# The low-rank projections of the attention at the head of a two-block kernel, on the raw input

## The chip, the cores and the metric

The kernel runs on one core of a Trainium2 chip. The metric is the time of one execution on the device in microseconds; the number to compare is the median of several executions.

## The reference, cut to what matters

The input `x` has 512 tokens of 1024 features in fp32. A first block holds a gated delta rule, latent attention and a feed-forward part; a second block holds a state space layer and a short convolution. Only the head of the first block bears on the change:

```
h = rmsnorm(x, norm_mix_g)                 # x * rsqrt(mean(x*x) + 1e-6) * g
z = h @ w_in
qkv_a, gate_a, a_a, b_a, c_q, c_kv, k_pe, gate_br_a, gate_br_b = split_in(z)
qkv_a = silu(causal_dwconv(qkv_a))         # delta rule: q, k, v of 8 heads
...                                        # chunked, with a triangular solve
cq  = rmsnorm(c_q,  mla_q_norm_g)          # 384 wide
q_b = cq @ w_uq
ckv = rmsnorm(c_kv, mla_kv_norm_g)         # 256 wide
kv  = ckv @ w_ukv
```

`rmsnorm` multiplies each token (row) by one factor. `c_q` and `c_kv` go through a second `rmsnorm` of their own, and a factor that is common to a row cancels there but for the `1e-6` under the root.

## The kernel before, in words

Activations are kept transposed, features on the partitions and the 512 tokens on the free axis, as tiles of 128x512. A product of 1024 input features to 128 output features is eight blocks of weights; since fp32 is split into a high and a low part (`hi`, `lo`), each block costs three matmuls `hi,hi`, `lo,hi`, `hi,lo`, 24 for a product, which add up in one PSUM bank. TensorE has four such banks for products (tiles `mm`) and four for everything else (`pt`). Weights come as chunks of eight blocks in exactly the order of the products (`order`, `pack_weights`): a chunk is loaded into `raw`, ScalarE writes its `hi`, VectorE or GpSimd its `lo`.

Each engine works off its own queue in order. The order is fixed when the program is built: tasks written as generators are advanced by `drive`, and `idle` hands some operations to VectorE or to GpSimd by an estimated clock. The product order is a hand-written table: `START`, then a few fixed products, then `GDN_ORDER`. In it `kq` is the k and q product of a delta-rule head, `vg` its v and gate, `bra` and `brb` two gates of the merge, `low` the three `cq` and two `ckv` products, `att` a head of the attention, `wv` its values, `ya` the first product behind the delta rule.

At the start the row factor `rs` of the first norm isn't known until all eight tiles of `x` have come. So the first products work on `x * gain` ("folded", `self.fold`), and what leaves PSUM is multiplied by `rs`: one VectorE operation `z<-mm,rs` for each product, behind which the convolution of a k or q product follows (one ScalarE and three VectorE operations), and then silu. `t_rs` computes `rs` (`meanrs`, `bcast`) and normalises the eight tiles (`x<-x,rs`), which are split again (`hi<-x,gmix` on ScalarE, `lo<-x,gmix,hi` on VectorE). From `unfold` on the products use these. The four products of `START` go block by block side by side, so they finish together. `ab` holds the decay and beta of the delta rule and the rotary key; `t_gates` runs a softplus on it (`sp_*`, `gg`), whose result TensorE sums (`pt<-gg,sqc`).

In a head of the delta rule `t_gdn_a` prepares k and q; for four heads together `t_solve` inverts triangular 32x32 blocks in 31 steps of two operations (`st<-sl,sx`, `sx<-sx,st`), in groups of four steps of which each goes to VectorE or to GpSimd; `t_gdn_b` carries the state through the four chunks of 128 tokens, from the tile `X` on, and ends in the tile `ga`. `ya` needs all eight `ga`.

`low` makes the five products from normalised tiles and copies each out of PSUM (`lr<-mm`, ScalarE); `t_rank_norm` then squares, adds and normalises them.

## Time and profile before

| | us |
|---|---|
| median of 3 runs | 1483.94 (1483.07 to 1485.86) |
| the profiled execution | 1485.18 |
| its span, first to last instruction | 1483.2 |
| TensorE busy | 1449.1 (98%) |
| VectorE busy | 864.5 (58%) |
| ScalarE busy | 655.1 (44%) |
| GpSimd busy | 503.9 (34%) |

The page's chain of what ended last is TensorE for 85% and VectorE for 10% of the span. A matmul's busy time in the trace is longer than its share of the engine, since matmuls overlap; the distance between the starts of two says more.

### The profile page before, as it was taken

What the parts mean: (1) busy time and instruction counts of PE and PEld (TensorE: products, weight loads), DVE (VectorE), ACT (ScalarE), POOL (GpSimd) and SP (SyncE); (2) the same over time, 40 slices, a digit from 0 to 9 for tenths busy, and PEclk for the clock granted to TensorE, in tenths of its full rate; (3) what the DMA queues carried; (4) which work ended last, traced back from release to release, by engine and by line L of the source; (5) the groups of instructions that cost most, each with busy time, mean ns of one, the idle gap of its engine ahead of it and who ended that gap; (6) DMA issues with size and microseconds to landing.
All of it is one profiled execution on the core that took longest, in us unless ns stands there. A gap on an engine that the chain in (4) does not pass through costs nothing.

```text
span 1483.2 us, 18958 instructions
## 1 busy us (share of the span) xinstructions
PE 1449.1 (98%) x7084; PEld 1191.0 (80%) x7084; DVE 864.5 (58%) x1755; ACT 655.1 (44%) x1118; POOL 503.9 (34%) x284
## 2 busy tenths in 40 slices
PE   8699999999999999999999999999999999999998
PEld 6588788878888888888888888888787778878877
DVE  7978988798665454358441144346975564360073
ACT  4565345234566664345442244444544544442342
POOL 0213010201333424442654455544024435534421
PEclk9799999999999999999999999999999999999999
DMA  5144323331222224423333333333233433422322
GB/s 192 50 147 127 117 82 96 87 86 58 80 79 78 79 72 128 147 94 100 99 99 99 90 96 99 94 96 94 71 104 114 118 115 98 137 86 85 105 85 94
DMA packets 56890, 147.61 MB, mean 100 GB/s; under 512 B 15008, under 2 KB 15584, under 8 KB 56800
## 3 DMA queue, kind: packets, MB, share of 16 engines
q1 hardware_dynamic: 56800, 146.42, 32.6%
q8 instruction: 55, 0.90, 0.2%
q14 instruction: 35, 0.29, 0.1%
HBM read 139.48 MB, written 5.34 MB: 98 GB/s over the span
## 4 chain that ended last, share of the span: by engine, by line
PE 85%; DVE 10%; DMA 2%; issue 1%; POOL 1%; ACT 1%; SPq 0%; DVEq 0%; POOLq 0%; ACTq 0%
PE mm L243 76%; PE pt L243 9%; DVE lo L243 3%; DVE st L243 1%; DVE sx L243 1%; DVE k L243 0%; DVE q L243 0%; SPq L243 0%; DVE rq_u L243 0%; DVE mix L243 0%; DMA raw<-wstream 0%; DVE v L243 0%; DVE xr L243 0%; DVE x L243 0%; ACT hi L243 0%
## 5 line engine op out<-in xcount | busy, mean ns | idle before, releaser
L243 PE MATMUL mm<-hi,hi 128*128 128x512 f32 (+2 forms) x1872 | 744.9, 398 | 5.6 <-ACT hi L243 3.5
L243 PE MATMUL mm<-lo,hi 128*128 128x512 f32 (+2 forms) x1872 | 729.1, 390 | 8.6 <-DVE lo L243 8.6
L243 PE MATMUL mm<-hi,lo 128*128 128x512 f32 (+2 forms) x1872 | 728.8, 390 | 3.9 <-DVE lo L243 3.9
L243 POOL TENSOR_TENSOR lo<-raw,hi 128x1024 fp32r<-128x1024 f32 x149 | 358.8, 2408 | 580.4 <-ACT hi L243 559.7
L243 PEld LDWEIGHTS mm<-hi,lo 128*128 128x128 f32 x1872 | 353.7, 189 | 78.9 <-DVE lo L243 5.1
L243 PEld LDWEIGHTS mm<-hi,hi 128*128 128x128 f32 x1872 | 354.3, 189 | 76.6 <-ACT hi L243 6.7
L243 PEld LDWEIGHTS mm<-lo,hi 128*128 128x128 f32 x1872 | 354.6, 189 | 76.1 <-DVE lo L243 10.3
L243 ACT ACTIVATE hi<-raw 128x1024 fp32r<-128x1024 f32 (+1 forms) x230 | 242.2, 1053 | 225.3 <-PE mm L243 172.1
L243 DVE TENSOR_TENSOR lo<-raw,hi 128x1024 fp32r<-128x1024 f32 (+1 forms) x81 | 102.6, 1267 | 2.6 <-ACT hi L243 2.5
L243 DVE TENSOR_TENSOR sq<-sq,sq 128x512 f32<-128x512 f32 x43 | 32.6, 770 | 93.0 <-ACT sq L243 93.0
L243 DVE TENSOR_TENSOR xr<-xr,mm 128x512 f32<-128x512 f32 x24 | 16.5, 688 | 97.5 <-PE mm L243 97.5
L243 DVE TENSOR_TENSOR lo<-fu,hi 128x512 fp32r<-128x512 f32 x22 | 43.0, 1956 | 41.5 <-ACT hi L243 41.5
L243 DVE SCALAR_TENSOR_TENSOR fu<-mm,params,fu 128x510 f32<-128x510 f32 (+1 forms) x38 | 28.5, 749 | 62.6 <-ACT fu L243 61.9
L243 POOL TENSOR_TENSOR q<-q,row 128x512 f32<-128x512 f32 x8 | 10.4, 1294 | 157.9 <-PE pt L243 92.5
L243 ACT ACT_TABLE_LOAD x37 | 47.5, 1283 | 8.3 <-DVE xbc L243 2.6
L243 POOL TENSOR_TENSOR fu<-fg,fu 128x512 f32<-128x512 f32 x22 | 30.0, 1365 | 44.9 <-DVE fu L243 41.3
L243 DVE TENSOR_TENSOR lo<-scz,hi 128x512 fp32r<-128x512 f32 x8 | 15.8, 1969 | 32.7 <-ACT hi L243 32.7
L243 DVE TENSOR_TENSOR lo<-pt,hi 128x512 fp32r<-128x512 f32 (+3 forms) x32 | 15.6, 489 | 28.9 <-ACT hi L243 28.8
L243 DVE SCALAR_TENSOR_TENSOR fg<-mm,params,fg 128x510 f32<-128x510 f32 (+1 forms) x38 | 28.3, 744 | 6.2 <-ACT fg L243 5.5
L243 ACT ACTIVATE fg<-fg 128x512 f32<-128x512 f32 x22 | 13.9, 631 | 39.4 <-DVE fg L243 39.4
L243 POOL TENSOR_TENSOR xdd<-xd,dd 128x512 f32<-128x512 f32 x8 | 9.4, 1176 | 58.7 <-DVE xd L243 58.6
L243 DVE TENSOR_SCALAR row<-row,cmp 128x128 f32<-128x128 f32 x64 | 26.9, 487 | 0.0
(314 smaller groups left out, 1513.9 us busy)
## 6 DMA issues: line engine op xcount, KB each, us to landing
raw<-wstream SPq DMA_DIRECT2D x228, 512.0 KB, 3.6
row<-grow_d SPq DMA_DIRECT2D x16, 256.0 KB, 4.2
row<-crow_d SPq DMA_DIRECT2D x16, 256.0 KB, 4.8
x<-xT SPq DMA_DIRECT2D x8, 256.0 KB, 5.4
sbd<-gate SPq DMA_DIRECT2D x8, 256.0 KB, 2.1
sb<-sbd SPq DMA_DIRECT2D x8, 256.0 KB, 3.9
xr<-xT SPq DMA_DIRECT2D x8, 256.0 KB, 3.8
Ce<-crow_d SPq DMA_DIRECT2D x16, 128.0 KB, 4.8
```

The lines of the kernel that those rows point to most:

```text
L243: return f(*args, **kw)
```

## The change

The five products `cq` and `ckv` move to the very start and work on `x * gain`; they are copied out of PSUM without `rs`. Their norm gets `epsx`, the mean square of the input (with its epsilon) times `1e-6`, in place of `1e-6`, so that the missing factor cancels exactly. `ab` still gets `rs`. The k and q products of heads 0 to 2 come behind `unfold`, from normalised tiles, the first three side by side. `low` now only starts the two norms. `GDN_ORDER` is another one; the last products ahead of `ya` are the same set.

```
-START = ["ab", ("k", 0), ("q", 0), ("k", 1)]
-GDN_ORDER = [("brb", 0), ("vg", 0), ("kq", 3), ("brb", 1), ("brb", 2), ("kq", 4), ...
+START = ["ab", ("cq", 0), ("cq", 1), ("cq", 2)]
+FIRST = [("k", 0), ("q", 0), ("k", 1)]
+GDN_ORDER = [("brb", 0), ("kq", 3), ("brb", 1), ("brb", 2), ("kq", 4), ("brb", 3), ("vg", 0), ...
...
-    o = [START] + one([("q", 1), ("k", 2), ("q", 2)])
+    o = [START] + one([("ckv", 0), ("ckv", 1)]) + [FIRST] + one([("q", 1), ("k", 2), ("q", 2)])
...
-                    nc.vector.tensor_scalar(a, cs, 1.0 / n, eps, ALU.mult, ALU.add)
+                    if isinstance(eps, float):
+                        nc.vector.tensor_scalar(a, cs, 1.0 / n, eps, ALU.mult, ALU.add)
+                    else:
+                        nc.vector.scalar_tensor_tensor(a, cs, 1.0 / n, eps, ALU.mult, ALU.add)
...
     def t_rs(self, x, n, gain, keep, eng=None):
-        r = yield from self.meanrs(x, n, eng=eng)
+        nc = self.nc
+        a = yield from self.meansq(x, n, eng=eng)
+        r = yield from self.rsqrt(a, NC)
         self.rs = yield from self.bcast(r, "rs")
+        if not keep:
+            self.epsx = self.const.tile([128, NC], F32, name="epsx")
+            nc.vector.tensor_scalar(self.epsx, a, EPS, None, ALU.mult)
...
-        r = yield from self.meanrs(raw, 128 * n)
+        a = yield from self.meansq(raw, 128 * n, eps=self.epsx)
+        r = yield from self.rsqrt(a, NC)
...
+        raws = {"cq": [None] * 3, "ckv": [None] * 2}
+
         def low():
-            for key, n, gname in (("cq", 3, "mla_q_norm_g"), ("ckv", 2, "mla_kv_norm_g")):
-                raw = [None] * n
-                for m in range(n):
-                    ps = yield from self.linear((key, m), self.xh)
-                    self.spawn(self.t_rows(raw, m, ps, None, "lr"))
-                self.spawn(self.t_rank_norm(key, raw, gname))
+            for key, gname in (("cq", "mla_q_norm_g"), ("ckv", "mla_kv_norm_g")):
+                self.spawn(self.t_rank_norm(key, raws.pop(key), gname))
...
         ps = yield from self.linears(START, self.xh)
         self.spawn(t_ab(ps[0]))
-        yield from kq(0, ps[1], ps[2])
+        for m in range(3):
+            self.spawn(self.t_rows(raws["cq"], m, ps[1 + m], None, "lr"))
+        for m in range(2):
+            ps = yield from self.linear(("ckv", m), self.xh)
+            self.spawn(self.t_rows(raws["ckv"], m, ps, None, "lr"))
+        yield from self.unfold()
+        ps = yield from self.linears(FIRST, self.xh)
+        yield from kq(0, ps[0], ps[1])
...
         yield from kq(2)
-        yield from self.unfold()
```

Three places show how the queues move. First, TensorE and ScalarE at the end of `START`, which is `mm17` here; TensorE before (`mm59` is q of head 1, `mm14` is `ab`):

```order
L243 MATMUL mm17_137<-lo42_223,hi3_221 128x512
L243 MATMUL mm17_137<-hi39_209,lo3_231 128x512
L243 MATMUL pt53_346<-sqc_75,rs50_322 128x128 [waits DVE_49]
L243 MATMUL pt53_346<-sqc_75,rs50_322 128x128 x3
L243 MATMUL mm59_361<-hi18_138,hi4_262 128x512 [waits DVE_49,Activation_49]
L243 MATMUL mm59_361<-lo20_142,hi4_262 128x512
```

TensorE now (`mm56` is the first `ckv` product):

```order
L244 MATMUL mm17_137<-lo42_223,hi3_221 128x512
L244 MATMUL mm17_137<-hi39_209,lo3_231 128x512
L244 MATMUL mm56_348<-hi18_138,hi4_262 128x512 [waits Activation_49]
L244 MATMUL mm56_348<-lo20_142,hi4_262 128x512
L244 MATMUL mm56_348<-hi18_138,lo4_273 128x512
L244 MATMUL mm56_348<-hi22_146,hi4_262 128x512
L244 MATMUL mm56_348<-lo28_159,hi4_262 128x512
L244 MATMUL mm56_348<-hi22_146,lo4_273 128x512
L244 MATMUL pt57_363<-sqc_75,rs50_322 128x128 [waits DVE_49]
L244 MATMUL pt57_363<-sqc_75,rs50_322 128x128 x3
L244 MATMUL mm56_348<-hi26_154,hi4_262 128x512
```

ScalarE before, and now:

```order
L243 ACTIVATE hi5_295<-raw5_290 128x1024 [waits DMAHW1_49,DVE_49,PE_49]
L243 COPY rs54_351<-pt53_346 128x512 [waits PE_49]
L243 ACTIVATE hi6_364<-raw6_362 128x1024 [waits DMAHW4_49,DVE_49]
L243 ACTIVATE hi63_378<-x4_103,gmix_112 128x512 [waits DVE_49]
L243 ACTIVATE cmp_393<-gyb67_390 128x4x8 [waits DVE_49]
```

```order
L244 ACTIVATE hi5_295<-raw5_290 128x1024 [waits DMAHW1_49,DVE_49,PE_49]
L244 COPY lr53_343<-mm15_135 128x512 [waits PE_49]
L244 COPY lr54_345<-mm16_136 128x512 [waits PE_49]
L244 COPY lr55_347<-mm17_137 128x512 [waits PE_49]
L244 ACTIVATE hi6_358<-raw6_349 128x1024 [waits DMAHW2_49,DVE_49]
L244 COPY rs58_368<-pt57_363 128x512 [waits PE_49]
L244 ACTIVATE hi63_395<-x4_103,gmix_112 128x512 [waits DVE_49]
```

The transposes that spread `rs` (`pt<-sqc,rs`) stood directly behind `START` and stand six matmuls later now; the next product waited for VectorE to empty the bank of `ab`, and now for ScalarE's copy of `mm15`, a `cq` product. On ScalarE three copies and the `hi` of a chunk stand ahead of the copy of `rs`.

Second, the softplus of the gates. VectorE ahead of it before (`k74`, `q75`, `k78` are convolutions, `x4` to `x11` the tiles of the input, `lo86` belongs to the rotary key):

```order
L243 SCALAR_TENSOR_TENSOR k74_409<-z60_372,params_74,k74_409 128x509 [waits Activation_49]
L243 SCALAR_TENSOR_TENSOR k74_409<-z60_372,params_74,k74_409 128x510 [waits DVE_49]
L243 SCALAR_TENSOR_TENSOR k74_409<-z60_372,params_74,k74_409 128x511 [waits DVE_49]
L243 TENSOR_TENSOR x8_107<-x8_107,rs54_351 128x512
L243 SCALAR_TENSOR_TENSOR q75_414<-z61_374,params_74,q75_414 128x509 [waits Activation_49]
L243 SCALAR_TENSOR_TENSOR q75_414<-z61_374,params_74,q75_414 128x510 [waits DVE_49]
L243 SCALAR_TENSOR_TENSOR q75_414<-z61_374,params_74,q75_414 128x511 [waits DVE_49]
L243 SCALAR_TENSOR_TENSOR k78_426<-z62_376,params_74,k78_426 128x509 [waits Activation_49]
L243 SCALAR_TENSOR_TENSOR k78_426<-z62_376,params_74,k78_426 128x510 [waits DVE_49]
L243 SCALAR_TENSOR_TENSOR k78_426<-z62_376,params_74,k78_426 128x511 [waits DVE_49]
L243 TENSOR_TENSOR lo86_489<-rot77_424,hi80_448 64x512 [waits Activation_49]
L243 TENSOR_TENSOR lo87_492<-rot77_424,hi80_448 64x512
L243 TENSOR_SCALAR sp_s70_399<-sp_e69_398 128x32 [waits Activation_49]
```

VectorE now:

```order
L244 TENSOR_TENSOR x7_106<-x7_106,rs58_368 128x512
L244 SCALAR_TENSOR_TENSOR lo74_430<-x5_104,gmix_112,hi65_405 128x512
L244 TENSOR_TENSOR x8_107<-x8_107,rs58_368 128x512
L244 SCALAR_TENSOR_TENSOR lo81_462<-x6_105,gmix_112,hi75_432 128x512 [waits Activation_49]
L244 TENSOR_TENSOR x9_108<-x9_108,rs58_368 128x512
L244 TENSOR_SCALAR sp_s71_422<-sp_e70_421 128x32 [waits Activation_49]
```

TensorE at the sum of the gates, before (`mm95` is the first product from normalised tiles) and now (`mm88` to `mm90` are k and q of head 0 and k of head 1):

```order
L243 MATMUL mm90_523<-hi39_209,lo6_382 128x512
L243 MATMUL pt97_573<-gg88_513,sqc_75 128x32 [waits DVE_49,PE_49]
L243 MATMUL pt97_573<-gg88_513,sqc_75 128x32
L243 MATMUL mm95_567<-hi63_378,hi7_476 128x512 [waits Activation_49]
L243 MATMUL mm95_567<-lo64_380,hi7_476 128x512
L243 MATMUL mm95_567<-hi63_378,lo7_538 128x512 [waits DVE_49]
```

```order
L244 MATMUL mm89_511<-hi75_432,lo6_373 128x512
L244 MATMUL pt95_556<-gg82_483,sqc_75 128x32 [waits DVE_49,PE_49]
L244 MATMUL pt95_556<-gg82_483,sqc_75 128x32
L244 MATMUL mm90_512<-hi75_432,hi7_485 128x512 [waits Activation_49]
L244 MATMUL mm90_512<-lo81_462,hi7_485 128x512
L244 MATMUL mm90_512<-hi75_432,lo7_507 128x512 [waits DVE_49]
L244 MATMUL mm88_510<-hi80_457,hi7_485 128x512
```

Nine convolution operations stood directly ahead of the softplus (`sp_s`), and none does now; all convolutions of heads 0 to 2 stand behind the split of the last input tile. On TensorE the sum stood ahead of the first product from normalised tiles and now stands behind 24 matmuls of it.

Third, GpSimd at the first solve, before and now (`q194` is a q tile, `X218` and `X228` are tiles `X`, `lo17` and `lo24` chunks of weights):

```order
L243 TENSOR_TENSOR st192_1250<-sl188_1202,sx189_1203 64x112 [waits Pool_49]
L243 TENSOR_TENSOR sx189_1203<-sx189_1203,st192_1250 64x28x4 [waits Pool_49]
L243 TENSOR_TENSOR lo17_1268<-raw17_1224,hi17_1259 128x1024 [waits DVE_49,DMAHW3_49,PE_49,Activation_49]
L243 MEMSET X218_1612 128x512
L243 MEMSET X228_1647 128x512
L243 TENSOR_TENSOR q194_1276<-q194_1276,row224_1637 128x512 [waits DMAHW3_49,PE_49,Activation_49]
```

```order
L244 TENSOR_TENSOR st194_1360<-sl190_1316,sx191_1317 64x112 [waits Pool_49]
L244 TENSOR_TENSOR sx191_1317<-sx191_1317,st194_1360 64x28x4 [waits Pool_49]
L244 TENSOR_TENSOR st194_1360<-sl190_1316,sx191_1317 64x247 [waits DVE_49,Pool_49]
L244 TENSOR_TENSOR sx191_1317<-sx191_1317,st194_1360 64x19x13 [waits Pool_49]
L244 TENSOR_TENSOR st194_1360<-sl190_1316,sx191_1317 64x252 [waits Pool_49]
L244 TENSOR_TENSOR sx191_1317<-sx191_1317,st194_1360 64x18x14 [waits Pool_49]
L244 TENSOR_TENSOR st194_1360<-sl190_1316,sx191_1317 64x255 [waits Pool_49]
L244 TENSOR_TENSOR sx191_1317<-sx191_1317,st194_1360 64x17x15 [waits Pool_49]
L244 TENSOR_TENSOR st194_1360<-sl190_1316,sx191_1317 64x256 [waits Pool_49]
L244 TENSOR_TENSOR sx191_1317<-sx191_1317,st194_1360 64x16x16 [waits Pool_49]
L244 TENSOR_TENSOR lo24_1535<-raw24_1517,hi24_1524 128x1024 [waits DMAHW3_49,PE_49,Activation_49]
L244 TENSOR_TENSOR st194_1360<-sl190_1316,sx191_1317 64x231 [waits DVE_49,Pool_49]
```

GpSimd did four of the 31 steps of each solve before; in the first it does sixteen now, handing over to VectorE and back, and in the second fifteen. Over the whole program VectorE has 46 solve operations fewer and GpSimd 46 more, and three of the `lo` operations on chunks pass from VectorE to GpSimd too. The k and q products of head 3, the last that the first solve needs, were the 11th and 12th product and are the 14th and 15th; from the last matmul of that q to the first matmul on a tile `X` there were 278 rows of TensorE and are 292. Ahead of `ya`, the last transposes of a delta-rule head (`pt<-sqc,X`) stood 100 rows of TensorE ahead of the first matmul of `ya`, and stand 40 rows ahead of it now.

## Rows read from the trace of the kernel before

**Rows 1.** Windows: length; busy us (count) of TensorE, loads, VectorE, ScalarE, GpSimd; granted clock.
```profile
31.00:80.00 49.00, 34.39 (x128) 26.80 (x127) 40.22 (x76) 28.37 (x63) 8.76 (x6) 0.76 0.18 53
80.00:450.00 370.00, 367.06 (x2051) 306.10 (x2050) 298.58 (x845) 169.59 (x412) 65.78 (x57) 1.00 0.32 96
```

**Rows 2.** What TensorE waited for, 31 to 80 us: total, times, longest.
```profile
PE mm L243 <- DVE lo L243: 7.4, 3, 3.7
PE pt L243 <- DVE gg L243: 4.7, 1, 4.7
PE mm L243 <- DVE ab L243: 2.1, 1, 2.1
```

**Rows 3.** Timeline of TensorE, 30 to 89 us: start, length, instruction, idle before it.
```profile
30.92 0.39 PE L243 MATMUL mm<-hi,lo 128*128 128x512 f32 x1
...
49.58 0.39 PE L243 MATMUL mm<-hi,hi 128*128 128x512 f32 x1
49.80 0.39 PE L243 MATMUL mm<-lo,hi 128*128 128x512 f32 x1
...
65.24 0.63 PE L243 MATMUL mm<-lo,hi 128*128 128x512 f32 x1
65.67 0.63 PE L243 MATMUL mm<-hi,lo 128*128 128x512 f32 x1
...
79.90 0.39 PE L243 MATMUL mm<-hi,hi 128*128 128x512 f32 x1
...
87.39 1.05 PE L243 MATMUL pt<-k 128*128 128x128 f32 x8
88.20 0.48 PE L243 MATMUL mm<-hi,hi 128*128 128x512 f32 x1
```

**Rows 4.** Timeline of VectorE, 33 to 63 us.
```profile
33.04 0.69 DVE L243 TENSOR_TENSOR x<-x,rs 128x512 f32<-128x512 f32 x1 [1.36 <-ACT rs L243]
...
50.29 2.31 DVE L243 SCALAR_TENSOR_TENSOR k<-z,params,k 128x509 f32<-128x509 f32 x3
...
53.93 0.18 DVE L243 TENSOR_SCALAR sp_s<-sp_e 128x32 f32<-128x32 f32 x1
...
57.57 0.74 DVE L243 SCALAR_TENSOR_TENSOR lo<-x,gmix,hi 128x512 fp32r<-128x512 f32 x1
...
61.67 1.22 DVE L243 TENSOR_TENSOR lo<-raw,hi 128x1024 fp32r<-128x1024 f32 x1
62.80 0.75 DVE L243 SCALAR_TENSOR_TENSOR lo<-x,gmix,hi 128x512 fp32r<-128x512 f32 x1
```

**Rows 5.** VectorE's groups by form, 31 to 76 us: count, busy us, mean ns, idle before.
```profile
L243 DVE TENSOR_TENSOR z<-mm,rs 128x512 f32<-128x512 f32 x6 | 3.9, 684 | 1.7 <-PE mm L243 1.7
```

**Rows 6.** Instructions on the tile lr: count, shortest, median, longest ns, first and last start.
```profile
L243 ACT COPY lr<-mm x5: 586/588/607, 314.4 to 359.1; 128x512 f32<-128x512 f32 x5
```

**Rows 7.** Timeline of GpSimd, at the rotary key and the first solve.
```profile
37.45 2.23 POOL L243 TENSOR_TENSOR rot<-kp,rope 128x512 f32<-128x512 f32 x1 [35.88 <-DMA kp<-ab]
...
42.11 1.30 POOL L243 TENSOR_TENSOR rot<-rot,swap 128x512 f32<-128x512 f32 x1
...
133.62 0.42 POOL L243 TENSOR_TENSOR sx<-sx,st 64x112 f32<-64x112 f32 x1
134.00 2.38 POOL L243 TENSOR_TENSOR lo<-raw,hi 128x1024 fp32r<-128x1024 f32 x1
```

**Rows 8.** Timeline of VectorE at the same solve.
```profile
134.07 2.46 DVE L243 TENSOR_TENSOR st<-sl,sx 64x135 f32<-64x135 f32 x1 [3.33 <-POOL sx L243]
...
149.46 0.42 DVE L243 TENSOR_TENSOR st<-sl,sx 64x256 f32<-64x256 f32 x1
```

**Rows 9.** What TensorE waited for, 80 to 450 us.
```profile
PE pt L243 <- DVE X L243: 0.9, 2, 0.6
```

**Rows 10.** Timeline of VectorE at the end of the delta rule.
```profile
419.62 0.75 DVE L243 SCALAR_TENSOR_TENSOR ga<-pt,params,ga 128x512 f32<-128x512 f32 x1 [0.81 <-PE pt L243]
...
448.08 4.91 DVE L243 TENSOR_TENSOR lo<-ga,hi 128x512 fp32r<-128x512 f32 x8 [2.22 <-ACT hi L243]
```

More of the change, by code (lines that the diff above doesn't have):

```diff
@@ L26 @@
 MFF = 22
-START = ["ab", ("k", 0), ("q", 0), ("k", 1)]
-GDN_ORDER = [("brb", 0), ("vg", 0), ("kq", 3), ("brb", 1), ("brb", 2), ("kq", 4), ("brb", 3), ("brb", 4), ("brb",
-             5), ("vg", 1), ("kq", 5), ("brb", 6), ("vg", 2), ("kq", 6), ("kq", 7), ("vg", 3), ("bra", 0),
-             ("brb", 7), ("vg", 4), ("vg", 5), ("vg", 6), ("low",), ("bra", 1), ("bra", 2), ("vg", 7), ("bra",
-             3), ("att", 0), ("wv", 0), ("att", 1), ("bra", 4), ("bra", 5), ("bra", 6), ("bra", 7), ("ya", 0),
+START = ["ab", ("cq", 0), ("cq", 1), ("cq", 2)]
+FIRST = [("k", 0), ("q", 0), ("k", 1)]
+GDN_ORDER = [("brb", 0), ("kq", 3), ("brb", 1), ("brb", 2), ("kq", 4), ("brb", 3), ("vg", 0), ("brb", 4), ("vg",
+             1), ("vg", 2), ("kq", 5), ("kq", 6), ("kq", 7), ("vg", 3), ("vg", 4), ("brb", 5), ("brb", 6),
+             ("brb", 7), ("vg", 5), ("vg", 6), ("low",), ("bra", 0), ("bra", 1), ("bra", 2), ("vg", 7), ("att",
+             0), ("bra", 3), ("wv", 0), ("att", 1), ("bra", 4), ("bra", 5), ("bra", 6), ("bra", 7), ("ya", 0),
              ("att", 2), ("ya", 1), ("att", 3), ("wv", 1), ("ya", 2), ("att", 4), ("ya", 3), ("att", 5), ("ya",
-             4), ("att", 6), ("ya", 5), ("att", 7), ("ya", 6), ("ya", 7)]
+             4), ("att", 6), ("att", 7), ("ya", 5), ("ya", 6), ("ya", 7)]
 PAIR_FFN = 3
@@ L115, in order @@
         elif item[0] == "low":
-            o += one([("cq", m) for m in range(3)] + [("ckv", m) for m in range(2)])
+            pass
         elif item[0] == "wv":
@@ L1432, in block1 @@
         self.spawn(t_ab(ps[0]))
-        yield from kq(0, ps[1], ps[2])
+        for m in range(3):
[6 more added lines that the diff above has]
+        yield from kq(0, ps[0], ps[1])
         d = {}
-        self.spawn(t_conv(d, "k", 1, 8, ps[3], self.fold))
+        self.spawn(t_conv(d, "k", 1, 8, ps[2], self.fold))
         del ps
@@ L1449, in block1 @@
             elif item[0] == "low":
-                yield from low()
+                low()
             elif item[0] == "wv":
```

## Prediction

> **What bounds the kernel now.** I read the busy time by stage first. From 80 to 450 us TensorE is busy for 367.1 of 370 us at the full clock, so a change there has 2.9 us of idle time to win at most. From 31 to 80 us it is busy for 34.4 of 49 us only, at a mean granted clock of 0.76, while VectorE is busy for 40.2 [rows 1]. The waits of this stretch name VectorE for nearly all the idle time: 7.4 us for split tiles (`lo`), 4.7 for the gates' `gg`, 2.1 for `ab` [rows 2]. So VectorE bounds the stage that the change rebuilds, and TensorE all that follows.
>
> The loss there comes from the timeline of TensorE. `START` ends at 30.92 + 0.23 = 31.15 us, and the 96th matmul of 512 columns after it (three folded products and the first from normalised tiles) starts at 79.90: 48.75 us. At the full clock two such matmuls start 0.22 to 0.23 us apart, so 96 take 21.8 us; eight transposes take 0.81 us (87.39 to 88.20), so the 24 and the few short matmuls between take about 3.2 [rows 3]. 48.75 - 21.8 - 3.2 = 23.8 us are lost. 14.6 of these are idle (49 - 34.4), and some 9 are time at the lower clock of 1.2 GHz, which TensorE shows behind its waits: there two starts are 0.43 us apart [rows 3].
>
> The timeline of VectorE shows why. It has the factor `rs` at 33.04, but normalises and splits the eight tiles among nine convolution operations (each three of them 2.31 us); the softplus runs from 53.93 to 57.57 only, and splits stand behind it [rows 4].
>
> **What the change removes there.** Six multiplications by `rs` fall away on VectorE, 6 x 0.68 = 4.1 us, 3.9 by the row [rows 5]; `ab` keeps its own. The bank of the next product is freed by a ScalarE copy of 0.59 us, known from the same products later on [rows 6], and not by VectorE behind `rs`. That copy's product (`mm15`) has its last matmul six starts, 1.4 us, ahead of the end of `START`, so the bank is free when TensorE gets there: the wait of 2.1 us goes.
>
> What is late next is `rs` itself. Its transposes now stand six matmuls later (1.4 us), and three copies and one `hi` stand ahead of its own copy on ScalarE. The ScalarE queue is through with those about when the transposes end. I take 0.9 us of delay: the first normalised tile at 33.9 and not 33.04 [rows 4].
>
> From there I add up VectorE's queue in its new order by lengths from rows: tiles of `x` 0.69, their `lo` 0.75, the `lo` of a chunk 1.13 (61.67 to 62.80), softplus 3.64 (53.93 to 57.57) [rows 4]. I put the first steps of the gates at 1.5 us. One chunk's `lo` needs ScalarE's `hi` only and is through at 34.1. Four operations of 512 (three tiles and `ab`, 2.8), one split (0.75), the gates (1.5), three tiles and two splits (3.6) bring the softplus to its start at 42.7 and to its end at 46.3; a split, a tile and the next chunk's `lo` (2.6) end at 48.9.
>
> TensorE has two `ckv` products with two sets of transposes until then, 31.15 + 10.9 + 1.3 = 43.3. Now each normalised tile serves nine matmuls (2.04 us) and not three, since three products run side by side, so tiles are asked for at a third of the pace. The sum of the gates is asked for after 24 matmuls, at 48.8 (2.5 us behind the softplus), that chunk's `lo` at 50.0, and the last tile at about 58.4, by the same adding up with some two us to spare. So in my sum no wait is left; the smallest margin is 1.1 us.
>
> GpSimd eats into it. Its rotary key operation took 2.23 us where a like one took 1.30, and VectorE's first solve operation took 2.46 us beside a GpSimd `lo` of 2.38, where a much wider one takes 0.42 [rows 7, 8]. The three rotary operations now fall on the tiles between 38 and 46 us. I put this at 1 us of waiting on TensorE with the clock kept; the bounds are 0 and 4 (the longest wait of that stretch, 3.7 [rows 2]). The nine convolutions come behind the last split, in the time of the next products, where they delay silu but no split.
>
> So the opening gives back 23.8 - 1 = 22.8 us (19.8 to 23.8).
>
> **What it moves.** The five products are the same work on TensorE wherever they stand; weights are packed anew, with as many chunks in the same pace, and no transfer is added. On SP chunk 7 now stands ahead of four swaps of the rotary key; nothing of it is late in my sum. `epsx` and two operations of other form are small, at about 0.17 us, and lie beside full TensorE time.
>
> The delta rule gets more GpSimd: 46 solve operations. No row shows one of the long ones on GpSimd. With 112 elements one takes 0.42 us there, and with 256 VectorE takes 0.42 [rows 7, 8]. If GpSimd's time doesn't grow with size, the bound is 0.42; if it grows in proportion, 0.96. I take 0.65, between them, since an operation on GpSimd with no small cost of its own is unlikely: 46 x 0.23 = 11 us more, some 5 for each solve. VectorE is relieved of 46 x 0.4 = 18 us. TensorE asks for the first `X` 292 rows behind q of head 3 and not 278, which is about 3 us of respite. TensorE waited 0.9 us for `X` in all [rows 9], so there is little slack: I put 2 us of new waits on it (bounds: a gain of all 2.9 us of idle time, or a loss of 12).
>
> Before `ya` the last head ended at 420.4 and its split at 448 or later, over 27 us of margin [rows 10]. 60 rows fewer lie between, at 0.23 us some 14 us, so half of it is left. VectorE in all has 338.8 of 419 us of work from 31 to 450 us [rows 1]; it loses 4 + 18 + three chunk splits of 1.1, about 25 us, while the stretch shrinks by 21, so it is no fuller.
>
> Sum: 22.8 - 2 = 20.8 us. The profiled span 1483.2 becomes 1462.4, and its time, 1.98 us more, 1464.4. The median of the three runs lay 1.2 us below the profiled execution, so 1463.
>
> **Against it.** The Trainium skill, in "SBUF — State Buffer", section "Who interferes with whom", says that a VectorE instruction with both inputs in SBUF and a GpSimd instruction that reads SBUF exclude each other for a whole instruction. Rows 7 and 8 agree in the one pair that they show, 2.46 us beside 2.38. By that rule each solve operation on GpSimd could wait out one of VectorE's, and the reverse.
>
> **The rivals.**
> - *The middle takes half.* The solves or the norms of `cq` and `ckv` come later and cost 8 to 12 us, TensorE's clock included. For it: the X waits have no slack [rows 9], and GpSimd's share of the solve triples and more. Against: the interval grew by 14 rows and VectorE is relieved. It gives 1484 - 23 + 10 = 1471.
> - *The opening only moves its loss.* The nine convolutions and the nine of q1, k2 and q2 all fall into the stretch behind the last split. 18 at 0.77 are 14 us of VectorE in some 20 us, beside the first decays and two chunks. If splits of chunks wait there as they did, most of the 23.8 us come back, and it ends at 1481 to 1487. Against: these are queued one product apart, and from 80 us on VectorE ran at 298.6 of 370 us without making TensorE wait [rows 1].
> - *Slower.* If each of the 46 operations waits as the rotary one did, 2.23 - 1.30 = 0.93 us [rows 7], both solves together are 43 us late. With X asked for on time that stands on TensorE: 1484 - 23 + 43 = 1504. It decides from 23 us of new waits on, half a microsecond for each operation. For it: the one pair in rows 7 and 8. Against: VectorE's operations out of PSUM are many in this stretch, and the four steps on GpSimd before ran at 0.42.
>
> **Chances.** The forecast 0.67, the half 0.20, the moved loss 0.06, slower 0.07. The forecast has a range of its own of 1459 to 1468. The range goes down by idle time that the middle may save and up through the half: 1457 to 1476, which leaves out some 0.17. A change of 0.2% (3 us) is about what a measurement of this kernel tells from none. Faster: 0.67 + 0.20 + 0.01 = 0.88; same 0.05; slower 0.07.
>
> **What the profile after would show.** TensorE between 31 and 60 us without a wait over 1 us and the granted clock at 1 from 34 us on; no `z<-mm,rs` for k and q; VectorE's softplus ending by 48 us; the 96th matmul behind `START` at 54 to 58 us and not 79.9; waits from 60 to 430 us at 3 to 7 us. I would be wrong if VectorE were late for a chunk's `lo` near 50 us and the clock fell, if X were waited for at 160 to 180 us, or if `ya` waited for the last head.

## The result and the profile after

The changed kernel takes 1473.22 us (median of 4 runs, 1471.44 to 1477.88), the kernel before 1483.84 beside it (4 runs): a ratio of 0.9926, 95% interval 0.9913 to 0.9939, so 10.6 us or 0.7% faster. The profiled execution took 1473.28 us with a span of 1471.5. The range of the prediction holds it. Its point, 1463, is 10 us too low, and the measured time lies outside the forecast's own range of 1459 to 1468. It is the time of the rival "the middle takes half" (1471).

The window of the opening after, with the columns of [rows 1]: TensorE is full and at the full clock.

```profile
31.00:80.00 49.00, 47.55 (x231) 38.89 (x230) 43.07 (x94) 32.34 (x73) 13.36 (x9) 1.00 0.35 104
```

What TensorE waited for from 31 to 80 us (against [rows 2]: 14.2 us in all):

```profile
PE mm L244 <- DVE lo L244: 1.2, 1, 1.2
PE pt L244 <- DVE gg L244: 0.3, 1, 0.3
```

The timeline of TensorE in the opening. `START` ends with the row at 30.47; the last row is the 96th product of 512 columns behind it, the 192nd in all. Before, that one started at 79.66 us: one start ahead of the row at 79.90 in [rows 3], which the prediction had counted as the 96th.

```profile
30.47 0.39 PE L244 MATMUL mm<-hi,lo 128*128 128x512 f32 x1
...
48.44 0.60 PE L244 MATMUL pt<-gg,sqc 128*128 128x32 f32 x4 [0.29 <-DVE gg L244]
...
50.74 0.50 PE L244 MATMUL mm<-hi,lo 128*128 128x512 f32 x1 [1.16 <-DVE lo L244]
...
55.64 0.39 PE L244 MATMUL mm<-hi,lo 128*128 128x512 f32 x1
```

VectorE in the opening (against [rows 4]): the first normalised tile, the softplus from 41.69 to `gg`, which starts at 48.08 and ends at 48.29, the chunk's `lo` that TensorE waits for.

```profile
33.69 0.69 DVE L244 TENSOR_TENSOR x<-x,rs 128x512 f32<-128x512 f32 x1
...
41.69 0.17 DVE L244 TENSOR_SCALAR sp_s<-sp_e 128x32 f32<-128x32 f32 x1
...
48.08 0.21 DVE L244 SCALAR_TENSOR_TENSOR gg<-gy,gea 128x32 f32<-128x32 f32 x1
...
49.47 1.22 DVE L244 TENSOR_TENSOR lo<-raw,hi 128x1024 fp32r<-128x1024 f32 x1
```

VectorE at the end of the delta rule (against [rows 10]): the last head, and the split that `ya` begins with.

```profile
418.32 0.74 DVE L244 SCALAR_TENSOR_TENSOR ga<-pt,params,ga 128x512 f32<-128x512 f32 x1
...
435.83 4.90 DVE L244 TENSOR_TENSOR lo<-ga,hi 128x512 fp32r<-128x512 f32 x8 [2.23 <-ACT hi L244]
```

So the 192nd product came 24.0 us earlier and the split 12.25 us earlier (448.08 - 435.83). What was won in the opening was half lost between these two rows. I call the time between them **the middle**: 448.08 - 79.66 = 368.4 us before, 435.83 - 55.64 = 380.2 after. 16 transposes of k and q moved into it (1.6 us by [rows 3]), so the loss is 380.2 - 368.4 - 1.6 = 10.2 us. Behind the split nothing of note changed: the profiled execution ends 1037.10 us behind it in the kernel before, and 1037.45 in the kernel after.

The windows of the two middles, before and after, with the columns of [rows 1]:

```profile
79.66:448.08 368.42, 365.48 (x2043) 304.82 (x2042) 296.67 (x841) 168.01 (x412) 65.78 (x57) 1.00 0.32 96
```
```profile
55.64:435.83 380.19, 371.85 (x2060) 310.53 (x2059) 302.59 (x816) 184.00 (x450) 106.49 (x107) 0.98 0.32 94
```

TensorE is idle for 8.3 us of it (380.19 - 371.85) and was for 2.9, so 5.4 of the 10.2 us are waits. The other 4.8 us are longer busy time (371.85 - 365.48 - 1.6); the granted clock is below 1.00 in a few stretches of the middle after, and in none of the middle before.

The largest waits after (80 to 450 us, against [rows 9]), and the windows around its stretches with a low clock:

```profile
PE pt L244 <- DVE X L244: 3.0, 4, 1.8
PE pt L244 <- DVE T L244: 2.8, 3, 2.1
```
```profile
170.00:180.00 10.00, 8.82 (x68) 6.35 (x67) 9.38 (x19) 2.21 (x4) 0.58 (x2) 1.00 0.53 158
185.00:190.00 5.00, 5.00 (x27) 4.41 (x25) 1.87 (x7) 1.07 (x6) 0.00 (x0) 0.66 0.20 79
320.00:330.00 10.00, 7.58 (x74) 6.16 (x72) 9.09 (x27) 2.65 (x5) 2.34 (x1) 0.76 0.43 147
330.00:340.00 10.00, 10.00 (x59) 9.15 (x58) 4.71 (x21) 2.04 (x12) 0.00 (x0) 0.73 0.01 2
```

Around 170 and 320 us three heads of the delta rule run their 64x64 products side by side, VectorE is busy for nine tenths with their transposes and copies, and behind the waits the granted clock falls, which it never did in the middle before.

A busy VectorE isn't enough to explain this. The kernel before had three heads side by side behind the second solve too (`X,T` at 320.8, 323.0 and 324.4 us), and its VectorE was as busy or busier behind both solves. What differs as well is how many products of 512 columns stand beside the heads. These are the 20 us from the first `X,T` behind each solve: two rows of all engines, then two of TensorE's products of 512 columns alone (busy us, count, clock); first before, then after.

```profile
175.53:195.53 20.00, 19.16 (x142) 15.40 (x143) 19.03 (x61) 7.88 (x22) 3.02 (x3) 1.00 0.37 114
320.77:340.77 20.00, 19.21 (x165) 15.66 (x165) 15.87 (x45) 5.23 (x19) 0.00 (x0) 1.00 0.27 84
...
175.53:195.53 20.00, 10.76 (x38) 1.00 0.37 114
320.77:340.77 20.00, 9.04 (x31) 1.00 0.27 84
```
```profile
172.60:192.60 20.00, 18.34 (x155) 15.01 (x156) 14.51 (x41) 5.05 (x17) 2.35 (x1) 0.91 0.29 86
315.88:335.88 20.00, 17.57 (x134) 14.60 (x134) 15.51 (x48) 3.41 (x10) 2.34 (x1) 0.74 0.30 86
...
172.60:192.60 20.00, 7.34 (x21) 0.91 0.29 86
315.88:335.88 20.00, 5.82 (x18) 0.74 0.30 86
```

Before, 38 and 31 dense products stood there and VectorE was busy for 19.0 and 15.9 us; after, it is 21 and 18 products, with VectorE busy for 14.5 and 15.5 us. The counts over longer stretches show where the others went. This is TensorE's products of 512 columns up to the first `X,T` product behind the first solve, and from the first behind the second on to the split; first before, then after:

```profile
0.00:175.53 175.53, 138.39 (x552) 0.92 0.40 126
...
320.77:448.08 127.31, 98.64 (x385) 1.00 0.25 74
```
```profile
0.00:172.60 172.60, 152.29 (x639) 1.00 0.46 140
...
315.88:435.83 119.95, 81.15 (x319) 0.96 0.22 66
```

87 products more are done before the first head goes on, but it goes on only 2.9 us earlier; 66 fewer are left behind the second solve.

### The profile page after: what moved, and what is told of

Same layout as the page of the kernel before. It is cut to its first block, busy times and chain, and to the rows that moved or that the text cites. A ratio compares the mean times of both kernels' runs of the same rounds, so it can differ in the third digit from the quotient of the medians.

```text
span 1471.5 us, 18957 instructions
## 1 busy us (share of the span) xinstructions
PE 1444.7 (98%) x7084; PEld 1188.1 (81%) x7084; DVE 854.4 (58%) x1701; ACT 657.8 (45%) x1120; POOL 542.6 (37%) x333
## 4 chain that ended last, share of the span: by engine, by line
PE 79%; DVE 13%; POOL 3%; issue 2%; ACT 1%; DMA 1%; SPq 1%; DVEq 0%; POOLq 0%; ACTq 0%
PE mm L244 71%; PE pt L244 8%; DVE lo L244 3%; POOL st L244 1%; POOL sx L244 1%; DVE st L244 1%; DVE sx L244 1%; DVE mix L244 1%; SPq L244 1%; ACT hi L244 0%; DVE Y L244 0%; DVE rq_u L244 0%; DVE qrs L244 0%; DMA x<-xT 0%; DVE v L244 0%
## 5 line engine op out<-in xcount | busy, mean ns | idle before, releaser
L244 POOL TENSOR_TENSOR lo<-raw,hi 128x1024 fp32r<-128x1024 f32 x152 | 365.2, 2403 | 536.4 <-ACT hi L244 509.0
L244 DVE TENSOR_TENSOR lo<-raw,hi 128x1024 fp32r<-128x1024 f32 (+1 forms) x78 | 97.4, 1249 | 3.5 <-ACT hi L244 3.5
L244 POOL TENSOR_TENSOR q<-q,row 128x512 f32<-128x512 f32 x8 | 10.6, 1319 | 96.6 <-PE pt L244 86.8
L244 POOL TENSOR_TENSOR st<-sl,sx 64x247 f32<-64x247 f32 (+15 forms) x31 | 20.8, 672 | 34.3 <-DVE sx L244 25.0
```

The lines of the kernel that those rows point to most:

```text
L244: return f(*args, **kw)
```

## The experiments

Each run gives its median, its ratio to the kernel before with the 95% interval, and in its trace the two rows that bound the middle, found by counting as above. The ratio is to the runs of the kernel before that were made beside it; their medians were 1483.84 to 1486.27 us. The middle can be compared where medians can't, since the opening varies by 2 us between executions of one order (last section).

| run | median us (runs) | ratio to before | 192nd product, split | middle |
|---|---|---|---|---|
| before | 1483.84 (4) | | 79.66, 448.08 | 368.4 |
| after | 1473.22 (4) | 0.9926 [0.9913, 0.9939] | 55.64, 435.83 | 380.2 |
| e1_old_table | 1490.77 (8) | 1.0039 [1.0025, 1.0052] | 55.58, 454.14 | 398.6 |
| e2_table_alone | 1523.79 (4) | 1.0257 [1.0239, 1.0275] | 79.22, 476.54 | 397.3 |
| e3_solve_vector | 1481.18 (11) | 0.9976 [0.9967, 0.9984] | 58.48, 444.48 | 386.0 |
| e4_b_two | 1480.90 (7) | 0.9972 [0.9960, 0.9984] | 57.36, 443.48 | 386.1 |
| f1_solve_back | 1483.70 (12) | 0.9994 [0.9981, 1.0006] | 55.19, 443.89 | 388.7 |
| f2_copies_act | 1470.48 (5) | 0.9909 [0.9895, 0.9923] | 57.77, 435.72 | 378.0 |
| f3_lo_vector | 1474.17 (5) | 0.9928 [0.9916, 0.9940] | 55.02, 435.66 | 380.6 |
| f4_both | 1471.28 (5) | 0.9911 [0.9896, 0.9926] | 57.35, 432.79 | 375.4 |
| g1_third_apart | 1485.57 (12) | 0.9997 [0.9986, 1.0008] | 57.11, 445.66 | 388.6 |
| g2_copies_replan | 1472.11 (5) | 0.9900 [0.9884, 0.9917] | 55.60, 431.79 | 376.2 |
| g4_no_cover | 1488.98 (12) | 1.0016 [1.0005, 1.0028] | 68.76, 452.51 | 383.8 |
| h1_short_solve | 1473.80 (6) | 0.9916 [0.9901, 0.9932] | 56.16, 434.44 | 378.3 |

**The change in halves.** Theory "table": the new order of products costs the 10 us. Theory "solve": the solves' operations on GpSimd do.

```diff
 # e1_old_table: the kernel after with
-GDN_ORDER = [("brb", 0), ("kq", 3), ("brb", 1), ...
+GDN_ORDER = [("brb", 0), ("vg", 0), ("kq", 3), ...   # as before
 # e2_table_alone: the kernel before with
-GDN_ORDER = [("brb", 0), ("vg", 0), ("kq", 3), ...
+GDN_ORDER = [("brb", 0), ("kq", 3), ("brb", 1), ...  # as after
```

> The kernel after with the table of products (GDN_ORDER) of the kernel before; the opening stays as changed, and the planner again gives GpSimd 66 operations of the two solves (64 after, 18 before). Theory "table": what the middle lost (TensorE idle 8.3 us of 80 to 450 us against 2.9 before, and about 4.7 us more at a granted clock below 1.00) comes from the new table, which lets three heads of the delta rule run their small products side by side. It then expects the idle time back near 3 us, the clock at 1.00, and 1473.2 - 9 = about 1464 us. Theory "solve": the loss comes from the solves' operations on GpSimd, which are here too: 1473 us, with the drops of the clock still there.

> The kernel before with the new table alone; START, the six z multiplications and the place of the low-rank projections in the middle stay as before, and 56 operations of the solves go to GpSimd. Theory "table": the middle loses its 9 to 10 us on top of the old opening, about 1493 us, with a drop of the granted clock between 170 and 350 us. Theory "solve": nearly the same, since the planner moves 38 of the 46 operations here as well: about 1492 us. If it stays at 1484 us, neither holds by itself, and it is the early low-rank results, which stand in the activation buffers, that the middle pays for.

Neither theory gave these numbers. With the old table the middle grows by 18 us; the new table on the old opening costs 29 us more than before. In e1 one wait behind the second solve is the largest, in the timeline of TensorE:

```profile
319.80 1.11 PE L244 MATMUL pt<-sqc,X 128*128 128x128 f32 x4 [9.13 <-DVE X L244]
```

So the new table by itself isn't what the middle pays for: with the new opening it saves 18 us, with the old one it costs 29. In both runs the planner made the rest of the order anew, and the two halves of the change don't have prices that add up.

**The solves.** First with the planner free, then with the order held: in the f runs the planner's choice of the next step is replaced by the list of steps that it chose in the kernel after, so that TensorE's order is the same row for row and only what is edited moves.

```diff
 # e3_solve_vector
-            eng = self.idle(4000, 2000, POOL_BIAS)
+            eng = nc.vector if j0 else nc.gpsimd
 # f1 to f4, order held
-            best = None
...
+        for n in STEPS:
+            self.advance(next(t for t in self.tasks if t["id"] == n))
 # f1_solve_back: the solves' entries in the list of engines, 1 for GpSimd
-1,0,0,1,0,1,1,0  0,0,1,1,1,0,0,1
+1,0,0,0,0,0,0,0  1,0,0,0,0,0,0,0
```

> The kernel after with the solves' engine fixed: the first four steps of each on GpSimd, the rest on VectorE (18 operations on GpSimd as before, 64 after). Theory "solve": the 9 us of the middle come back, about 1464 us. Theory "table": no gain, 1473 us within 2 us, and the waits for T and X around 326 us and before the first ya product stay.

> The kernel after, with the order of all engines' steps held as the planner made it there (the planner is replaced by its own list of steps), and 46 operations of the solves moved back from GpSimd to VectorE: 16 of the 62 on GpSimd, as before; TensorE's order is the same row for row. Theory "solve costs" (GpSimd and VectorE stopping each other in the solves is what the middle pays): 5 to 9 us faster than after, 1464 to 1468 us. Theory "solve helps" (the move takes 46 x 0.42 = 19 us from a VectorE that is the late engine): slower than after by 3 to 19 us, 1476 to 1492 us.

"Solve costs" fell, and "solve helps" gave the time of f1. The time of e3 is in the range of neither of its theories. With the operations back on VectorE the middle is 8.5 us longer with the order held, and 5.8 with a new one. The windows of f1 at the end of the first solve show VectorE full in the first and TensorE idle for 5.3 of 20 us; 3.72 of them are one wait for the first `X`, and the first `X,T` starts at 177.60 us and not at 172.60:

```profile
160.00:170.00 10.00, 8.38 (x38) 6.59 (x37) 9.48 (x29) 2.12 (x3) 0.00 (x0) 1.00 0.21 59
170.00:180.00 10.00, 6.28 (x38) 4.55 (x37) 6.82 (x14) 4.92 (x9) 3.79 (x4) 0.93 0.37 94
```

In after, GpSimd's groups over both solves stand at 672 and 591 ns, near the 0.65 that I had estimated for the moved ones:

```profile
L244 POOL TENSOR_TENSOR st<-sl,sx 64x247 f32<-64x247 f32 (+15 forms) x31 | 20.8, 672 | 34.3 <-DVE sx L244 25.0 <-DMA sl<-ldram 3.7 <-DVE rq_u L244 3.5
L244 POOL TENSOR_TENSOR sx<-sx,st 64x247 f32<-64x247 f32 (+15 forms) x31 | 18.3, 591 | 2.4
```

The Trainium skill, "Perfetto Trace Analysis", section "Optimizing Scalar/DVE Operations", says that moving work from a saturated VectorE to GpSimd may make sense, and warns that it might not help because the two share a port. Here it helps, by 5.8 (e3) to 8.5 us (f1) of the middle.

**Three heads at once.** Theory "bunch": the third head beside the first two is what makes VectorE late.

```diff
 # e4_b_two
-LIMIT = {"a": 2, "b": 3, ...
+LIMIT = {"a": 2, "b": 2, ...
 # g1_third_apart
-("vg", 1), ("vg", 2), ("kq", 5), ("kq", 6),
+("vg", 1), ("kq", 5), ("vg", 2), ("kq", 6),
```

> The kernel after with at most two heads of the delta rule's second half at a time (three before and after); 48 operations of the solves on GpSimd. Theory "table" (three heads side by side make VectorE late and leave TensorE with small products alone): the drop of the clock near 326 us goes, waits in the middle fall to some 4 us, 1466 to 1468 us. Theory "solve": 48 operations instead of 64, a gain of a third of the loss at most, 1470 us. Against both: fewer heads side by side leave each head's own chain of VectorE steps uncovered, and the time rises above 1475 us.

> The kernel after with one place of the table changed: the products of kq5 stand between vg1 and vg2, so that the second half of the third head starts some 10 us behind the first two, as in the kernel before (X,T at 176, 178 and 209 us there, at 173, 174 and 177 us after); the planner makes the rest anew. Theory "bunch" (three heads at once leave TensorE with 64x64 products between VectorE's steps, and its clock falls): no drop of the clock at 185 to 190 us, the waits of 172 to 184 us gone, 2 to 4 us faster than after, 1469 to 1471 us. Theory "later heads" (what stands after the first solve runs late anyway, and a head put back only moves the waits to 200 to 260 us, as with two heads at a time): 1474 to 1480 us.

In both the drop of the clock near 187 us is gone, and the middles of both are longer than that of after, by 5.9 and 8.4 us. The windows of e4:

```profile
250.00:260.00 10.00, 6.51 (x56) 5.43 (x55) 9.51 (x39) 3.41 (x7) 2.30 (x3) 1.00 0.02 8
260.00:270.00 10.00, 7.98 (x37) 6.39 (x37) 5.95 (x27) 2.20 (x8) 3.64 (x9) 0.66 0.45 138
```

From 250 to 270 us only 8 products of 512 columns run in e4, and VectorE is the full engine in the first half of it. So "bunch" fell. What was said against both theories gave the time of e4. "Later heads" had the direction of g1, but not its size: 1485.57 us against 1474 to 1480, and its longest wait, 3.86 us for an `X`, stands at 305 us and not at 200 to 260.

**VectorE relieved, order held.** Two suspected causes of VectorE's lateness in the bunches are taken away, one by one and together: its own copies out of PSUM, and what GpSimd's subtractions of weight chunks hold up.

```diff
 # f2_copies_act (f4_both has it too)
-            nc.vector.tensor_copy(xe[odd(a), :, a, 0], q4(p)[side(a), :, a])
+            nc.scalar.copy(xe[odd(a), :, a, 0], q4(p)[side(a), :, a])
-        nc.vector.tensor_copy(self.v4(Y)[0:64, :, 64:128], half(p)[0:64])
+        nc.scalar.copy(self.v4(Y)[0:64, :, 64:128], half(p)[0:64])
-                    nc.vector.tensor_copy(st2, p[:, 0:128])
+                    nc.scalar.copy(st2, p[:, 0:128])
 # f3_lo_vector (f4_both has it too): the engine of three chunks' lo, at 323.2, 410.6 and 414.1 us
-1  1  1
+0  0  0
```

> The kernel after, order of steps held, with the copies out of PSUM of the delta rule's second half (X and Y of each head, the first state) on ScalarE instead of VectorE: 32 copies, 10 us of VectorE between 170 and 420 us, most of it in the two stretches where three heads run side by side. Theory "VectorE is late in the bunches": waits for X, T and Y at 172 to 184 us and 321 to 327 us shrink to 1 us or less, the clock stays up, 1466 to 1469 us. Theory "stops" (VectorE is late only where GpSimd's subtraction of a weight chunk holds it): the waits at 326 and 417 us stay, no more than 2 us are gained, 1471 to 1473 us.

> The kernel after, order of steps held, with three subtractions of weight chunks (those at 323.2, 410.6 and 414.1 us on GpSimd, 2.34 to 2.40 us each) on VectorE, where one takes 1.21 us. Theory "stops": the 1.25, 2.34 and 2.81 us operations of VectorE beside them fall to 0.2 to 0.7 us, the waits of 2.10 us at 326 and 1.83 us at 417 go to under 1 us, and with the clock that stays up some 4 us are gained, 1469 us. Theory "VectorE is late in the bunches": the 1.21 us that VectorE does itself eats what it saves, 1473 us within 1.5 us.

> The kernel after, order of steps held, with both edits: the 32 copies on ScalarE and the three subtractions on VectorE. If both theories hold in part, the gains add up: 1464 to 1467 us. If neither does and the waits are set by the order of TensorE's own queue (heads' products put ahead of dense ones that could have run), it stays at 1472 us, and the waits only change their name.

The copies alone shorten the middle by 2.2 us: the clock no longer falls at 187 us, but a wait of 2.20 us for `T` at 326 us stays and it falls there. The subtractions alone do nothing (380.6): the longest wait for `T` goes from 2.1 to 1.0 us, but the clock falls at both places as before. Together they give 4.8 us, more than the sum. In the windows of f4 VectorE has more room at both places, the clock is nearly kept, and TensorE gets more done in the same time (82 and 70 matmuls of any size from 320 to 340 us, 74 and 59 in after). The first row is its middle:

```profile
57.35:432.79 375.44, 368.53 (x2060) 307.45 (x2059) 293.33 (x787) 192.19 (x479) 99.34 (x104) 1.00 0.32 95
170.00:180.00 10.00, 9.24 (x72) 7.10 (x70) 8.65 (x16) 2.78 (x6) 2.26 (x4) 1.00 0.57 140
185.00:190.00 5.00, 4.58 (x34) 3.92 (x33) 1.40 (x4) 2.62 (x11) 0.00 (x0) 1.00 0.34 105
320.00:330.00 10.00, 8.88 (x82) 7.05 (x81) 6.57 (x22) 5.14 (x13) 0.00 (x0) 0.88 0.34 100
330.00:340.00 10.00, 10.00 (x70) 9.29 (x70) 5.19 (x24) 3.48 (x20) 0.00 (x0) 0.95 0.12 45
```

Of the 4.8 us only 1.4 are waits (TensorE is idle for 6.9 us of its middle, 8.3 in after); 3.3 are shorter busy time. In place of waits for VectorE there are now waits for `X`, `gst` and `T` from ScalarE, 2.8 us in all. The wait for the last head's `X` stays (1.64 us in f4, 1.83 in after), so GpSimd wasn't its cause, though "stops" had said so of f3.

By time the expectations did less well. f2 lies between the ranges of its two theories. f3 is where "VectorE is late in the bunches" had it. f4 isn't at the 1464 to 1467 us of gains that add up, but at the 1472 that was expected if the waits only change their name. By the medians f2 and f4 gain 2 to 3 us on after, and the intervals overlap with that of after; what I rest on is the middle of one profiled execution each. In that of f4 the 4.8 us of the middle are 2.0 us of the whole time, since its opening ended 1.7 us later than that of after and 1.0 us was lost behind the split. That after and f3 have 380.2 and 380.6 with TensorE in the same order is all there is on how well a middle repeats.

**The same copies with a new order.** The edit is the three copies of the diff above, in the kernel after; the planner is free again.

> The kernel after with the 32 copies on ScalarE as in f2_copies_act, but with the planner free to order the steps for it (there the order was held, 2.5 us faster than after). If the planner's own reckoning follows the chip, it does not get worse: 1466 to 1470 us. If what an order is worth hangs on where three heads meet a chunk of weights that is not split yet, any new order can lose 5 us and more by that alone: 1475 us or above, with a drop of the granted clock at another place.

The middle is 376.2 us, and the granted clock stays at 1.00 from 31 to 450 us. TensorE is still idle for 8.3 us of the middle (376.19 - 367.84), as in after: with the clock kept, the waits remain. The time, 1472.11 us, lies between the two ranges that were expected. At 0.9900 [0.9884, 0.9917] its ratio is the lowest of all kernels here, though its interval overlaps with that of after.

**The cover of the opening.**

```diff
 # g4_no_cover
-    o = [START] + one([("ckv", 0), ("ckv", 1)]) + [FIRST] + one([("q", 1), ("k", 2), ("q", 2)])
+    o = [START, FIRST] + one([("q", 1), ("k", 2), ("q", 2), ("ckv", 0), ("ckv", 1)])
```

> The kernel after without the cover of the opening: ckv0 and ckv1 (48 products of 512 columns, 10.2 us) stand behind k2 and q2 instead of between START and the three projections of the normalised tiles; the planner makes the rest anew. Theory "cover" (START's sum of squares, its root and the first normalised tile are late until about 40 us, and only the two ckv projections hide that): TensorE waits some 8 to 10 us at 31 to 41 us, for the row factor and the first split tile, its clock falls there, and the time is 1482 to 1488 us. Theory "order alone" (the gain of the opening is that nothing of k and q is multiplied by the row factor out of PSUM, and the place of ckv is of no account): 1473 us within 3 us.

"Cover" holds in the main: the 192nd product starts 13.1 us later than in after, and the time is 1 us above the range of this theory. Of the waits that it named, the one for the row factor is 0.4 us only and the one for the first split tile 2.2; the gates' `gg` (3.1) and `ab` (2.0) are waited for too. The waits and the window of g4 (31 to 80 us, 31 to 50 us):

```profile
PE pt L244 <- DVE gg L244: 3.1, 1, 3.1
PE mm L244 <- DVE lo L244: 2.2, 1, 2.2
PE pt L244 <- DVE ab L244: 2.0, 1, 2.0
```
```profile
31.00:50.00 19.00, 11.28 (x36) 8.71 (x36) 17.02 (x36) 7.91 (x13) 7.76 (x6) 0.72 0.29 83
```

Taking the factor out of k and q isn't enough: 13.1 of the 24.0 us hang on 10 us of products that need neither the factor nor the gates, and 10.9 us are left without this cover.

**Shorter solves.** The run leaves out 23 of the 31 steps of each solve.

```diff
 # h1_short_solve
-        for j0 in range(0, 31, 4):
+        for j0 in range(0, 8, 4):
```

> The kernel after with only the first two groups of four steps in each of the two solves (8 of 31 steps; what the other 23 add to sx is left out, so the output is not the reference's), the planner free. It shortens the chain that the heads wait for by some 30 us each time, and takes 46 operations from GpSimd and VectorE. Theory "chain" (after the opening TensorE is 24 us ahead, but the solves' ends and with them the heads move up by 3 to 5 us only, so that 87 products more are used up before the first X,T and too few are left to stand between the heads' small ones): the middle gives its loss back, waits of 80 to 450 us at 3 to 4 us, clock at 1.00, 1461 to 1465 us. Theory "order" (what is lost hangs on how the small products of three heads meet each other and the weight chunks, whenever they come): 1469 to 1476 us, with waits for X and T and a drop of the clock as in after.

The theory "chain" is not borne out by the time: 1473.80 us, in the range of "order", with the middle 1.9 us shorter. Its windows say why it isn't simply wrong. The losses at 130 to 200 us (TensorE idle for 0.0 us, 1.9 in after) and at 300 to 450 us (0.6, 5.3 in after) are gone, and a new one stands at 270 to 300, where a head starts by itself (`X,T` at 287.70), TensorE waits for its `T` and `X`, and the clock falls. Since the planner made a new order, the run doesn't settle what the length of the solves costs:

```profile
270.00:300.00 30.00, 25.54 (x138) 20.93 (x138) 18.26 (x55) 7.85 (x18) 5.71 (x4) 0.89 0.44 126
300.00:450.00 150.00, 149.40 (x827) 124.72 (x826) 103.89 (x268) 74.17 (x167) 39.94 (x21) 1.00 0.23 69
```

## Why the prediction was right, and where it was off

- **The opening: right in size and in its steps.** Forecast 22.8 us; measured 24.0 - 1.6 = 22.4, of which 0.45 lie ahead of the end of `START`. The first normalised tile came at 33.69 (33.9 forecast), the gates were asked for at 48.1 (48.8), the 96th product behind `START` came at 55.6 (54 to 58). GpSimd's rotary operations took more of VectorE than I had put: three operations of the softplus took 0.94, 1.15 and 0.61 us, 0.18 to 0.19 before, and each ends with one of GpSimd. So it ended at 48.3 and not 46.3, though it began 1 us earlier than I had summed, which was luck. The mark "by 48 us" was just missed, and the margin of 1.1 us at the chunk's `lo` became a wait of 1.16. The waits of 31 to 80 us, 1.45 in all, are near my 1 us of waiting. g4 shows that the cover by `ckv` carries 13.1 us of the gain.
- **The six multiplications: right.** No `z<-mm,rs` for k and q is left, and the wait for `ab` is gone.
- **The middle: the step that failed is the term "2 us of new waits on it". The new waits measured 5.4 us, and 4.8 us of longer busy time came with them, for which the sum had no term: 10.2 in all.** I had the term from the one wait for `X` [rows 9] and from VectorE's share over the whole stretch. The runs show in its place: TensorE waits for tiles of VectorE in short stretches behind the two solves, and the clock falls there. VectorE is nearly full for about 10 us at a time there whatever its mean is, but so it was before, beside 38 and 31 dense products and not 21 and 18. Relieving it with the order held gives 4.8 us back (f4), 1.4 of waits and 3.3 of busy time. Of the 5.4 us that are left, 4.0 are waits and 1.4 busy time; what causes them is open. The solves on GpSimd are not it (f1: they save 8.5), the table by itself is not (e1: it saves 18 with this opening), and shorter solves with a new order gave back 1.9 (h1). That fewer dense products stand beside the heads is seen in the counts, but no run held everything else and gave them back. Nor does a run test whether the five low-rank results, which now wait in their buffers from the opening on, cost something.
- **The solves' price: right, but it was put on the wrong side.** The operations took what I estimated; what they take from VectorE weighs more than their length, so the rival "slower", which let each stop cost TensorE, was far off. But VectorE was relieved by less than I put: its busy time in the whole program fell by 10.1 us (864.5 to 854.4), not by some 25. Its solve operations fell by 17.9 us, while others grew longer (`sof<-rq_u`: 161 ns on the mean before, 328 after).
- **The margin before `ya`: 27 us, half left, I said.** It is 435.83 - 419.06 = 16.8 us. `ya` doesn't wait for the last head; the wait of 1.83 us is inside that head.
- **The rivals.** "The middle takes half" had 0.20 and came, with TensorE's clock as it said. Its later solves came in one count only: the first `X,T` is 2.9 us earlier by the clock, but 21 us later counted from the 192nd product (117.0 us, 95.9 before), a time that dense products fill.
- **The signs of being wrong.** One came in part: the chunk's `lo` was late near 50 us, with the clock kept in after, though not in every execution (last section). Near 180 us `X` is waited for by 0.46 us. The waits from 60 to 430 us came to 8.3 us and not to 3 to 7.

## What to carry to other kernels

This opening, which waited for one engine, could be added up row by row to within a microsecond. What such an opening wins must then be followed to the next place where a chain, not TensorE, sets the pace: work brought forward is work that no longer stands beside that chain (here this is seen in the counts, and not isolated by a run). A share of busy time over hundreds of microseconds hides stretches of ten in which the engine is full; read windows as short as the burst of work that follows a release, read the same windows of the kernel before, and count the dense work in both. Where a planner makes the order, test an edit with the order held: with a new order going back to the old table moved this middle by 18 us, and shifting one entry of the table moved it by 8.4.

## What the hardware showed that I had not expected

**One wait, two clocks.** In after and in f2, which have the same order up to there, TensorE waits 1.16 and 1.15 us for the same `lo` near 51 us. In after the granted clock stays at 1.00; in f2 two starts are 0.43 us apart behind the wait, and the window shows the lower level of 1.2 GHz:

```profile
51.30 0.70 PE L244 MATMUL mm<-hi,lo 128*128 128x512 f32 x1 [1.15 <-DVE lo L244]
51.80 0.63 PE L244 MATMUL mm<-hi,hi 128*128 128x512 f32 x1
52.23 0.63 PE L244 MATMUL mm<-lo,hi 128*128 128x512 f32 x1
```
```profile
52.00:54.00 2.00, 2.00 (x6) 0.50 0.83 219
```

Of the eleven profiled executions with the opening of after, each of which waits 1.1 to 1.2 us for this `lo`, five show the drop (192nd product at 57.1 to 58.5 us), six don't (55.0 to 56.2). So this wait of a microsecond costs about 2 us more in some executions, and single runs of one kernel differ by that.

**A short operation held for a whole one.** All engines of after around 324 us: an operation of 4 elements a partition on VectorE, elsewhere 0.17 us, takes 1.25 and ends with GpSimd's subtraction (325.56); the copies out of PSUM and the transposes beside it keep their length.

```profile
323.08 0.56 DVE L244 COPY X<-pt 32x128 f32<-32x128 f32 x2
323.22 2.34 POOL L244 TENSOR_TENSOR lo<-raw,hi 128x1024 fp32r<-128x1024 f32 x1 [12.19 <-ACT hi L244]
...
323.67 0.64 DVE L244 STREAM_TRANSPOSE Y<-X 32x128 f32<-32x128 f32 x2
...
324.34 1.25 DVE L244 TENSOR_SCALAR rq_t<-ms_a 128x4 int32<-128x4 int32 x1
...
...
326.16 0.58 PE L244 MATMUL pt<-T,yodd 64*64 64x64 f32 x3 [2.10 <-DVE T L244]
```

By the Trainium skill, "SBUF — State Buffer", section "Who interferes with whom", a VectorE instruction of this kind can take the port that GpSimd uses, and the loser waits for the whole instruction; this row agrees, and the rows beside it show which instructions go free.
